# A decoder layer on one core: modulation and first latents in halves, earlier norms, later rope tables

## The chip, the cores and the metric

The kernel runs on one core of one Trainium2 chip. The metric is the time of one execution in device microseconds, from the first to the last instruction with the little that lies around them. The engines are PE (TensorE; PEld is its loading of weights), DVE (VectorE), ACT (ScalarE), POOL (GpSimd) and SP (SyncE, which issues most transfers).

## What is computed

One decoder layer on 512 rows of width 1024. The part that the change touches is the very beginning: six modulation vectors from a conditioning vector, a normed and modulated input, and the low-rank query latents of its projection.

```python
mod = silu(c) @ w_ada + b_ada                    # 6 vectors of 1024
shift1, scale1, gate1, shift2, scale2, gate2 = mod
h = rms_norm(x, norm1_g) * (1 + scale1) + shift1
proj = h @ w_in                                  # split: cq, ckv, kpe, fq, fk, fv, fl
q_a = rms_norm(cq, mla_qa_g) @ w_uq              # 8 heads, latent attention with rope
kv_a = rms_norm(ckv, mla_kva_g) @ w_ukv
# attention of both groups, o @ w_o, gate1, residual
# second norm and modulation, 8 heads of product keys, top 16 of 16384 experts, gate2, residual
```

## The kernel before

The 512 rows are four tiles of 128. Every tile's row block is transposed to eight blocks of 128 features, so a product with an input matrix runs over eight k blocks. Products that need accuracy are made of three (`mm3`, L380 to L387): both operands are split into an upper part in the fast float format and a lower part, the rest, and upper·upper, upper·lower and lower·upper are summed in one PSUM bank. `halves` (L364) loads a weight matrix in blocks of two k, casts the upper part on ACT (L373) and subtracts on DVE (L374).

The modulation is computed from `w_ada`, 512 columns at a time: `wload` (L283) loads a half vector's matrix in four blocks of 512 KB, `mod_parts` (L298) multiplies, and the second step of `mod_cols` (L307) turns the sums into columns, 4 of the 8 columns of `a1` (scale times gain) or `b1` (shift). So `a1` and `b1` come in two halves, each for four of the eight k blocks.

`hidden` (L400) makes one tile's modulated rows. Its first step loads x and norms it (`normed_T`, L340: Square on ACT with the sum, a reciprocal root on GpSimd, a scaling on DVE). Its second step transposes all eight blocks, applies `a1` and `b1` (`scaled`, L156: even blocks on ACT, odd ones on DVE) and splits the result (`part`, L393: upper part on ACT; lower part of blocks 0 to 3 on DVE, of 4 to 7 on GpSimd). `latent_q` (L412) multiplies with `w_c0` (384 columns, 24 products a tile) and norms; `latent_k` (L424) does it with `w_c1` (296 columns); then come `w_fv`, `w_fk`, `w_fq` (512 columns each).

The order is written out at the end of `build`: a list of steps (L1068), in which only tiles 0 and 1 are taken through `hidden`, then `tables` (L206), which calls `rope_tables` (L233), then `pipe` (L63) over the tasks, which starts one task a tick and resumes each three ticks later. Tiles 2 and 3 are the first two tasks. From this program order a scheduler makes a fixed list of instructions for each engine at build time; each engine then runs its list in order. It may put an instruction earlier in an engine's list than the program has it, if its inputs are there by the scheduler's own estimate.

Buffers: the pool `k4` (L93) has 28 slots of 4 KB a partition for x, the normed rows `xn`, the split rows `hT`, raw and split weights and the modulation's blocks; `ld` has 4, `k3` has 6, PSUM has 6 banks named `bank` and 2 named `bank2`. A transfer into a slot waits until the slot's former content has been used.

Of the kernel before, what the change touches and what calls it, by code (L numbers as in the profile page):

```python
# [17 lines left out]
OP = mybir.AluOpType  # L18
# [3 lines left out]
P = 128  # L22
S = 512
D = 1024
KD = D // P
# [53 lines left out]
class Layer:  # L79
# [75 lines left out]

    def scaled(self, dst, a, b=None):  # L156

        def f(j, n, p):
            for q in range(n):
                d, s, x = dst(j + q), p[:, q, :], j + q  # L160
                if x % 2:
                    if b is None:
                        self.nc.vector.tensor_scalar(d, s, a[:, x:x + 1], None, op0=OP.mult)
                    else:
                        self.nc.vector.tensor_scalar(d, s, a[:, x:x + 1], b[:, x:x + 1], op0=OP.mult, op1=OP.add)
                else:
                    self.nc.scalar.activation(d, s, AF.Identity, scale=a[:, x:x + 1],
                                              bias=0.0 if b is None else b[:, x:x + 1])
        return f
# [36 lines left out]
    def tables(self):  # L206
# [23 lines left out]
        self.logf = [cp.tile([P, H], F32, name=f"logf{i}") for i in range(NT)]  # L230
        self.rope_tables()

# [106 lines left out]

    def normed_T(self, dst, x, a, b):  # L340

        nc = self.nc
        h = self.k4([P, D], "xn")
        ss, rstd = self.sm([P, 1], "nss"), self.sm([P, 1], "nrs")
        nc.scalar.activation(h, x, AF.Square, accum_out=ss)
        self.rsqrt(rstd, ss, 1, 1.0 / D)
        nc.vector.tensor_scalar(h, x, rstd, None, op0=OP.mult)
        yield
        self.transposes([h[:, k * P:(k + 1) * P] for k in range(KD)], self.scaled(dst, a, b))
# [13 lines left out]

    def halves(self, name, src, raw, new):  # L364

        if name not in self.wt:
            kd, n = src.shape[1:]
            his, los = [], []
            for k in range(0, kd, 2):
                w = raw([P, 2, n], "w")  # L370
                self.last_load = self.nc.sync.dma_start(w, src[:, k:k + 2, :])
                hi, lo = new([P, 2, n], "whi", F32R), self.k4([P, 2, n], "wlo", F32R)
                self.nc.scalar.copy(hi, w)  # L373
                self.nc.vector.tensor_tensor(out=lo, in0=w, in1=hi, op=OP.subtract)  # L374
                his += [hi[:, x, :] for x in range(2)]
                los += [lo[:, x, :] for x in range(2)]
            self.wt[name] = his.__getitem__, los.__getitem__
        return self.wt[name]

    def mm3(self, pb, lhs, rhs, kd):  # L380

        pe = self.nc.tensor
        for k in range(kd):
            (lh, ll), (rh, rl) = (tuple(f(k) for f in t) for t in (lhs, rhs))
# [3 lines left out]

    def w_in(self, name):

        return self.halves(name, self.I[name], self.k4, self.ld if name in ("w_c1", "w_fk") else self.k4)

    def part(self, f, hl, engs):  # L393

        for q in range(0, KD, 4):
            hi, lo, src = (t[:, q:q + 4] for t in (*hl, f))
            self.nc.scalar.copy(hi, src)
            engs[q // 4].tensor_tensor(out=lo, in0=src, in1=hi, op=OP.subtract)

    def hidden(self, i, T):  # L400
        nc = self.nc
        x = self.k4([P, D], "x")
        self.load(x, self.I["x"][i * P:(i + 1) * P, :])
        f = x.rearrange("p (k t) -> p k t", k=KD)
        yield from self.normed_T(lambda k: f[:, k, :], x, self.mods["a1"], self.mods["b1"])
        T["hT"] = [self.k4([P, KD, P], "hT" + z, F32R) for z in "hl"]
        self.part(f, T["hT"], (nc.vector, nc.gpsimd))

    def times_h(self, pb, i, T, name):
        self.mm3(pb, [lambda k, z=z: T["hT"][z][:, k, :] for z in range(2)], self.w_in(name), KD)  # L410

    def latent_q(self, i, T):  # L412
        nc, v = self.nc, self.nc.vector
        pq = self.bank()
        self.times_h(pq[:, :QR], i, T, "w_c0")
        T["cl"] = cl = self.k3([P, QR + KVR], "cl")
# [580 lines left out]
    def build(self):  # L997
# [57 lines left out]
        def gates(i):  # L1055
# [3 lines left out]
        each = lambda f, *a: [f(i, T[i], *a) for i in every]  # L1059
        base = (each(self.latent_q) + each(self.latent_k) + each(self.fox_v) + each(self.fox_qk, 0)  # L1060
                + each(self.fox_qk, 1) + each(self.mla_tile))
        hs = [self.hidden(i, T[i]) for i in every]
        for x in ("a1", "b1", "a2", "b2"):
            self.mods[x] = self.cp.tile([P, KD], F32, name=x)
        m = [f for half in range(2) for f in (self.mod_cols(0, "b1", 0, None, True, (half,)),
                                              self.mod_cols(1, "a1", 1, 4, True, (half,)))]
        h0, h1 = hs[:2]
        for g in (m[0], h0, h1, m[1], m[0], m[2], m[1], m[3], m[2], m[3], h0, h1):  # L1068
            next(g, None)
        self.tables()  # L1070
        mods = spread(seq(self.mod_row(2, 0, self.g1d), self.mod_cols(3, "b2", 2), self.mod_cols(4, "a2", 3, 5),
                          self.mod_row(5, 1, self.g2d)), 2)
# [4 lines left out]
                    spread(q1(2), 2), top(0, 2))  # L1077
        tasks = hs[2:] + base + self.heads(0, T)
        skip = len(tasks) + 10
# [83 lines left out]
```

## Time and profile before

| | us |
|---|---|
| median of 3 runs | 1729.67 |
| lowest and highest | 1727.96, 1730.6 |
| the profiled execution | 1727.06 |
| its span, first to last instruction | 1725.3 |
| busy in the span: PE, DVE, ACT, POOL | 1594.3, 1251.7, 679.0, 470.3 |

A busy time is a sum of marks; PE's marks overlap, so a busy PE need not be at its peak. The granted clock is a share of 2.4 GHz: 1.00 is 2.4 GHz, 0.50 is 1.2 GHz. In rows of the timeline the start stands first, then the time, engine and line, the output and the input, and in brackets the engine's idle time before the row and what ended it. An engine's name with q (SPq, ACTq) is its issue of a transfer.

### The profile page before, as it was taken

What the parts mean: (1) busy time and instruction counts of PE and PEld (TensorE: products, weight loads), DVE (VectorE), ACT (ScalarE), POOL (GpSimd) and SP (SyncE); (2) the same over time, 40 slices, a digit from 0 to 9 for tenths busy, and PEclk for the clock granted to TensorE, in tenths of its full rate; (3) what the DMA queues carried; (4) which work ended last, traced back from release to release, by engine and by line L of the source; (5) the groups of instructions that cost most, each with busy time, mean ns of one, the idle gap of its engine ahead of it and who ended that gap; (6) DMA issues with size and microseconds to landing.
All of it is one profiled execution on the core that took longest, in us unless ns stands there. A gap on an engine that the chain in (4) does not pass through costs nothing.

```text
span 1725.3 us, 24991 instructions
## 1 busy us (share of the span) xinstructions
PE 1594.3 (92%) x8993; PEld 1398.1 (81%) x8993; DVE 1251.7 (73%) x2626; ACT 679.0 (39%) x1072; POOL 470.3 (27%) x506
## 2 busy tenths in 40 slices
PE   5999999888985999999999999689999999999996
PEld 2976498876985999999999999677777777777885
DVE  3524454476799888778878787488888788888863
ACT  3522364335321544334656565333333333333331
POOL 1203500000033345533112111133433234343421
PEclk8999999899996999999999999889999999999998
DMA  7355413347325888888999999899999999999963
GB/s 289 119 208 185 164 46 111 110 153 255 118 94 201 268 257 263 269 262 264 317 297 317 305 300 300 295 362 399 363 356 376 373 367 374 363 372 378 311 197 105
DMA packets 189904, 451.34 MB, mean 262 GB/s; under 512 B 16595, under 2 KB 102611, under 8 KB 185685
## 3 DMA queue, kind: packets, MB, share of 16 engines
q1 hardware_dynamic: 92884, 279.27, 45.8%
q0 software_dynamic: 38016, 137.38, 22.8%
q10 hardware_dynamic: 58880, 33.11, 6.4%
q8 instruction: 70, 1.15, 0.3%
q14 instruction: 54, 0.43, 0.1%
HBM read 393.07 MB, written 56.63 MB: 261 GB/s over the span
## 4 chain that ended last, share of the span: by engine, by line
PE 60%; DVE 4%; DMA 3%; ACT 1%; issue 1%; POOLq 0%; POOL 0%; DVEq 0%; ACTq 0%; SPq 0%
PE acc L978 30%; PE bank L934 9%; PE bank L933 9%; PE bank L932 9%; PE bank L817 2%; DMA G<-gst 1%; DVE ulo L869 1%; DMA ge<-ged 1%; ACT vhi L868 1%; DVE scr L846 0%; DMA gt<-G 0%; DVE idf L770 0%; DVE vlo L869 0%; DMA g<-g2d 0%; DMA x<-xd 0%
## 5 line engine op out<-in xcount | busy, mean ns | idle before, releaser
L978 PE MATMUL acc<-vhi,whl 128*128 128x512 f32 x1536 | 421.8, 394 | 38.5 <-ACT whl L968 20.0
L978 PEld LDWEIGHTS acc<-vhi,whl 128*128 128x128 f32 x1536 | 288.5, 189 | 107.2 <-ACT vhi L868 23.7
L932 PE MATMUL bank<-hhi,uhi 128*128 128x384 f32 x1024 | 345.7, 338 | 21.0 <-DMA hhi<-hd 17.5
L934 PE MATMUL bank<-hhi,ulo 128*128 128x384 f32 x1024 | 347.0, 339 | 9.8 <-DVE ulo L869 9.7
L933 PE MATMUL bank<-hlo,uhi 128*128 128x384 f32 x1024 | 347.9, 340 | 0.2 <-DMA hlo<-hd 0.2
L868 ACT CAST uhi<-ut 128x1024 fp32r<-128x1024 f32 x128 | 134.5, 1051 | 305.2 <-PE bank L933 297.7
L828 POOL DMA_INDIRECT gat<-in_peer_v,ids x128 | 158.7, 1240 | 343.6 <-DVE y L856 314.0
L828 POOL DMA_INDIRECT gat<-in_peer_u,ids x128 | 141.5, 1106 | 385.4 <-DVE sact L846 355.1
L978 PE MATMUL acc<-vlo,whl 128*128 128x512 f32 x768 | 240.8, 395 | 3.4 <-DVE vlo L869 3.4
L869 DVE TENSOR_TENSOR ulo<-ut,uhi 128x1024 fp32r<-128x1024 f32 x128 | 177.7, 1388 | 77.8 <-ACT uhi L868 77.7
L932 PEld LDWEIGHTS bank<-hhi,uhi 128*128 128x128 f32 x1024 | 193.9, 189 | 22.4 <-issue 17.6
L934 PEld LDWEIGHTS bank<-hhi,ulo 128*128 128x128 f32 x1024 | 194.0, 189 | 13.2 <-DVE ulo L869 12.9
L933 PEld LDWEIGHTS bank<-hlo,uhi 128*128 128x128 f32 x1024 | 193.9, 189 | 1.1 <-DMA hlo<-hd 0.7
L868 ACT CAST vhi<-vt 128x1024 fp32r<-128x1024 f32 x128 | 133.8, 1049 | 142.2 <-PE acc L978 126.2
L869 DVE TENSOR_TENSOR vlo<-vt,vhi 128x1024 fp32r<-128x1024 f32 x128 | 156.6, 1223 | 43.2 <-ACT vhi L868 42.8
L978 PEld LDWEIGHTS acc<-vlo,whl 128*128 128x128 f32 x768 | 144.6, 189 | 36.9 <-DVE vlo L869 5.6
L856 DVE SCALAR_TENSOR_TENSOR y<-gat,swgt,y 128x1024 f32<-128x1024 f32 x127 | 166.7, 1313 | 2.2 <-DMA gat<-in_peer_v,ids 2.1
L968 ACT CAST whl<-ge 128x384 fp32r<-128x384 f32 x128 | 65.2, 511 | 249.6 <-PE acc L978 224.9
L846 DVE CUSTOM_DVE_ANT_0 scr<-gat,h2r 128x1024 bf16<-128x1024 f32 x128 | 157.3, 1229 | 0.8 <-DMA gat<-in_peer_u,ids 0.8
L969 DVE TENSOR_TENSOR whl<-ge,whl 128x384 fp32r<-128x384 f32 x128 | 70.6, 556 | 51.4 <-ACT whl L968 51.2
L819 ACT ACTIVATE gst<-bank 128x512 f32<-128x512 f32 x96 | 96.7, 1115 | 0.1
L965 DVE TENSOR_TENSOR ge<-ge,gt 128x384 f32<-128x384 f32 x128 | 69.4, 554 | 23.3 <-DMA gt<-G 16.7
(251 smaller groups left out, 2232.9 us busy)
## 6 DMA issues: line engine op xcount, KB each, us to landing
ut<-in_peer_uT SPq DMA_DIRECT2D x128, 512.0 KB, 5.0
vt<-in_peer_v SPq DMA_DIRECT2D x128, 512.0 KB, 6.8
G<-gst ACTq DMA_DIRECT2D x24, 1024.0 KB, 9.9
gt<-G SPq DMA_DIRECT2D x16, 1536.0 KB, 9.5
ged<-ge SPq DMA_DIRECT2D x120, 192.0 KB, 4.3
ge<-ged SPq DMA_DIRECT2D x120, 192.0 KB, 6.9
w<-in_w_ada SPq DMA_DIRECT2D x16, 1024.0 KB, 7.2
w<-in_w_pq SPq DMA_DIRECT2D x32, 512.0 KB, 5.2
```

Source lines behind the costliest of these rows:

```text
L819: nc.scalar.activation(st[:, :, q + t4:q + t4 + 4].rearrange("p i t -> p t i"), pb.rearrange("p (t i) -> p t i", t=4), AF.Copy, scale=1.0 ...
L828: self.nc.gpsimd.indirect_dma_start(out=t, out_offset=None, in_=self.I[table], in_offset=bass.IndirectOffsetOnAxis(ap=ids[:, k:k + 1], axi ...
L846: v.tensor_tensor_reduce(out=scr, in0=u, in1=self.rows, op0=OP.mult, op1=OP.add, scale=1.0, scalar=0.0, accum_out=a[:, k:k + 1])
L856: v.scalar_tensor_tensor(out=self.y, in0=t, scalar=w[:, k:k + 1], in1=self.y, op0=OP.mult, op1=OP.add)
L868: nc.scalar.copy(hi, src)
L869: self.last_split = eng.tensor_tensor(out=lo, in0=src, in1=hi, op=OP.subtract)
L932: pe.matmul(A, uh[:, k, :], hh, start=(k == 0), stop=False)
L933: pe.matmul(A, uh[:, k, :], hl, start=False, stop=False)
L934: pe.matmul(A, ul[:, k, :], hh, start=False, stop=(k == KD - 1))
L965: nc.vector.tensor_tensor(out=wg, in0=wg, in1=self.gt[:, :, b % GI, :], op=OP.mult)
L969: nc.vector.tensor_tensor(out=wl, in0=w, in1=wh, op=OP.subtract)
L978: self.nc.tensor.matmul(self.acc[t][half], w[:, ts], v[:, half * 512:(half + 1) * 512], start=(b == n == 0), stop=(b == NK - 1 and n == 2))
```

## The change

Six things are changed. `hidden` has three steps: norm; transposes, modulation and split of blocks 0 to 3; the same of blocks 4 to 7. `latent_q` has its products in two steps, over k blocks 0 to 3 and 4 to 7, into the same bank. `w_in` can load just the first part of a matrix. The written order takes all four tiles through the norm beside the first half of the modulation, loads the first half of `w_c0` ahead of the second half of the modulation, does the first halves of all tiles' rows and latents before the second half of the modulation is turned into columns, and then the second halves. The lower part of the split is always taken on DVE (it was on GpSimd for blocks 4 to 7). `rope_tables` is no longer called in `tables`; it is a task of its own behind the latents. The number of tasks falls by one.

```diff
-    def scaled(self, dst, a, b=None):
+    def scaled(self, dst, a, b=None, k0=0):
@@ tables
         self.logf = [cp.tile([P, H], F32, name=f"logf{i}") for i in range(NT)]
-        self.rope_tables()
@@ halves
-    def halves(self, name, src, raw, new):
+    def halves(self, name, src, raw, new, upto=None):
...
+        his, los = self.wt[name]
+        if len(his) < (upto or kd):
+            for k in range(len(his), upto or kd, 2):
                 w = raw([P, 2, n], "w")
                 self.last_load = self.nc.sync.dma_start(w, src[:, k:k + 2, :])
...
@@ mm3
-        for k in range(kd):
+        for k in ks or range(kd):
...
@@ hidden
-        yield from self.normed_T(lambda k: f[:, k, :], x, self.mods["a1"], self.mods["b1"])
+        h = self.norm(x)
+        yield
         T["hT"] = [self.k4([P, KD, P], "hT" + z, F32R) for z in "hl"]
-        self.part(f, T["hT"], (nc.vector, nc.gpsimd))
+        for q in range(0, KD, 4):
+            self.transposes([h[:, k * P:(k + 1) * P] for k in range(q, q + 4)],
+                            self.scaled(lambda k: f[:, k, :], self.mods["a1"], self.mods["b1"], q))
+            hi, lo, t = (z[:, q:q + 4] for z in (*T["hT"], f))
+            nc.scalar.copy(hi, t)
+            nc.vector.tensor_tensor(out=lo, in0=t, in1=hi, op=OP.subtract)
+            yield
@@ latent_q
-        self.times_h(pq[:, :QR], i, T, "w_c0")
+        self.times_h(pq[:, :QR], i, T, "w_c0", range(KD // 2))
+        yield
+        self.times_h(pq[:, :QR], i, T, "w_c0", range(KD // 2, KD))
@@ build
-        h0, h1 = hs[:2]
-        for g in (m[0], h0, h1, m[1], m[0], m[2], m[1], m[3], m[2], m[3], h0, h1):
+        lq = [self.latent_q(i, T[i]) for i in every]
+        for g in (m[0], *hs[:2], m[1], *hs[2:], m[0], m[1]):
+            next(g, None)
+        self.w_in("w_c0", KD // 2)
+        for g in (m[2], m[3], *hs[:2], *lq[:2], *hs[2:], *lq[2:]):
+            next(g, None)
+        self.w_in("w_c0")
+        for g in (m[2], m[3], *hs):
             next(g, None)
         self.tables()
+        base = (lq + [prep(self.rope_tables)] + each(self.latent_k) + each(self.fox_v) + each(self.fox_qk, 0)
+                + each(self.fox_qk, 1) + each(self.mla_tile))
...
-        tasks = hs[2:] + base + self.heads(0, T)
+        tasks = base + self.heads(0, T)
```

## Rows read from the trace of the kernel before

**Rows 1.** The page's strip of 40 slices: busy tenths of PE
```profile
PE   5999999888985999999999999689999999999996
```

**Rows 2.** PE's waits from 0 to 45 us: total, times, longest
```profile
PE bank L385 <- ACT whi L373: 9.7, 1, 9.7
```

**Rows 3.** Stretches: length, busy PE, PEld, DVE, ACT, POOL, granted clock, DMA share, GB/s
```profile
20.00:31.20 11.20, 10.28 (x70) 4.32 (x68) 5.25 (x20) 4.30 (x9) 0.00 (x0) 1.00 1.03 407
31.00:32.00 1.00, 0.19 (x2) 0.10 (x1) 0.62 (x5) 0.37 (x2) 0.00 (x0) 0.78 1.05 410
31.20:40.80 9.60, 0.00 (x0) 0.00 (x0) 3.20 (x17) 5.72 (x13) 3.07 (x4) 0.52 0.40 140
40.80:48.70 7.90, 7.46 (x24) 6.63 (x25) 6.47 (x11) 4.91 (x10) 1.51 (x4) 0.50 0.31 90
48.70:63.50 14.80, 14.80 (x89) 14.77 (x89) 6.58 (x11) 5.45 (x14) 5.52 (x8) 1.00 0.30 94
63.50:76.60 13.10, 13.10 (x98) 13.10 (x98) 4.87 (x19) 6.62 (x21) 4.10 (x17) 1.00 0.64 238
110.00:200.00 90.00, 87.58 (x422) 57.58 (x422) 35.58 (x54) 23.96 (x38) 32.19 (x48) 1.00 0.59 216
```

**Rows 4.** Timeline from 20 to 45 us, single rows of several engines
```profile
20.10 2.77 PE L303 MATMUL bank<-w,c 128*32 128x512 f32 x20
20.69 1.67 SPq L281 DMA_DIRECT2D x<-in_x  x2
23.30 21.15 SPq L371 DMA_DIRECT2D w<-in_w_c  x6
24.35 0.81 ACT L167 ACTIVATE x<-bank,b,a 128x128 f32<-128x128 f32 x2 [1.71 <-DVE a L321]
27.12 0.69 DVE L398 TENSOR_TENSOR hTl<-x,hTh 128x512 fp32r<-128x512 f32 x1 [0.34 <-ACT hTh L397]
28.40 1.05 PE L303 MATMUL bank<-w,c 128*32 128x512 f32 x4 [0.23 <-DMA w<-in_w_ada]
29.50 0.33 ACTq L243 DMA_DIRECT2D rg<-in_rope_g  x1
31.63 0.81 ACT L167 ACTIVATE x<-bank,b,a 128x128 f32<-128x128 f32 x2 [1.55 <-DVE a L321]
35.34 0.23 DVE L276 SCALAR_TENSOR_TENSOR rope<-ropework,rg 128x64 f32<-128x64 f32 x1 [2.46 <-DMA rg<-in_rope_g]
36.87 1.14 ACT L397 CAST hTh<-x 128x512 fp32r<-128x512 f32 x2 [3.45 <-DVE x L165]
37.56 2.49 POOL L398 TENSOR_TENSOR hTl<-x,hTh 128x512 fp32r<-128x512 f32 x2 [22.28 <-ACT hTh L397]
37.91 1.05 ACT L345 ACTIVATE xn<-x 128x1024 f32<-128x1024 f32 x1
40.01 0.81 ACT L373 CAST whi<-w 128x768 fp32r<-128x768 f32 x1
40.87 1.01 PE L385 MATMUL bank<-whi,hTh 128*128 128x384 f32 x2 [9.69 <-ACT whi L373]
```

**Rows 5.** Timeline of PE from 45 to 64 us, single rows
```profile
45.59 0.52 PE L387 MATMUL bank<-whi,hTl 128*128 128x384 f32 x1
47.19 0.52 PE L387 MATMUL bank<-whi,hTl 128*128 128x384 f32 x1
52.89 1.04 PE L136 MATMUL bank<-ident,xn 128*128 128x128 f32 x8
60.91 0.34 PE L385 MATMUL bank<-whi,hTh 128*128 128x384 f32 x1
63.51 0.30 PE L385 MATMUL bank<-whi,hTh 128*128 128x296 f32 x1
```

**Rows 6.** SP's waits from 0 to 66 us, and issues from 44 to 48 us (median to landing)
```profile
SPq L371 <- POOL hTl L398: 11.6, 2, 10.5
...
w<-in_w_c SPq DMA_DIRECT2D x2, 296.0 KB, 2.8
```

More of the change, by code (lines that the diff above doesn't have):

```diff
@@ L154, in apart @@
         return f
-    def scaled(self, dst, a, b=None):
+    def scaled(self, dst, a, b=None, k0=0):
         def f(j, n, p):
             for q in range(n):
-                d, s, x = dst(j + q), p[:, q, :], j + q
+                d, s, x = dst(k0 + j + q), p[:, q, :], k0 + j + q
                 if x % 2:
@@ L338, in mod_row, with norm @@
         yield
-    def normed_T(self, dst, x, a, b):
+    def norm(self, x):
         nc = self.nc
@@ L347, in normed_T @@
         nc.vector.tensor_scalar(h, x, rstd, None, op0=OP.mult)
+        return h
+    def normed_T(self, dst, x, a, b):
+        h = self.norm(x)
         yield
@@ L362, in weights1 @@
         return self.wt[name, 1]
-    def halves(self, name, src, raw, new):
+    def halves(self, name, src, raw, new, upto=None):
+        kd, n = src.shape[1:]
         if name not in self.wt:
-            kd, n = src.shape[1:]
-            his, los = [], []
-            for k in range(0, kd, 2):
+            self.wt[name] = ([], [])
+        his, los = self.wt[name]
+        if len(his) < (upto or kd):
+            for k in range(len(his), upto or kd, 2):
                 w = raw([P, 2, n], "w")
@@ L376, in halves, with mm3 @@
                 los += [lo[:, x, :] for x in range(2)]
-            self.wt[name] = his.__getitem__, los.__getitem__
-        return self.wt[name]
-    def mm3(self, pb, lhs, rhs, kd):
+        return his.__getitem__, los.__getitem__
+    def mm3(self, pb, lhs, rhs, kd, ks=None):
         pe = self.nc.tensor
-        for k in range(kd):
+        for k in ks or range(kd):
             (lh, ll), (rh, rl) = (tuple(f(k) for f in t) for t in (lhs, rhs))
@@ L387, in mm3, with w_in @@
             pe.matmul(pb, ll, rh, start=False, stop=(k == kd - 1))
[L389 to L398, printed above, removed]
+    def w_in(self, name, upto=None):
+        return self.halves(name, self.I[name], self.k4, self.ld if name in ("w_c1", "w_fk") else self.k4, upto)
     def hidden(self, i, T):
@@ L404, in hidden, with times_h @@
         f = x.rearrange("p (k t) -> p k t", k=KD)
-        yield from self.normed_T(lambda k: f[:, k, :], x, self.mods["a1"], self.mods["b1"])
+        h = self.norm(x)
+        yield
         T["hT"] = [self.k4([P, KD, P], "hT" + z, F32R) for z in "hl"]
-        self.part(f, T["hT"], (nc.vector, nc.gpsimd))
-    def times_h(self, pb, i, T, name):
-        self.mm3(pb, [lambda k, z=z: T["hT"][z][:, k, :] for z in range(2)], self.w_in(name), KD)
+        for q in range(0, KD, 4):
[5 more added lines that the diff above has]
+            yield
+    def times_h(self, pb, i, T, name, ks=None):
+        self.mm3(pb, [lambda k, z=z: T["hT"][z][:, k, :] for z in range(2)], self.w_in(name, ks and ks[-1] + 1), KD, ks)
     def latent_q(self, i, T):
@@ L1059, in build @@
         each = lambda f, *a: [f(i, T[i], *a) for i in every]
-        base = (each(self.latent_q) + each(self.latent_k) + each(self.fox_v) + each(self.fox_qk, 0)
-                + each(self.fox_qk, 1) + each(self.mla_tile))
         hs = [self.hidden(i, T[i]) for i in every]
```

## The prediction

> **What bounds the kernel now.** I read the page first. Its strip of 40 slices has PE at nine tenths or more nearly everywhere after the first slice, so whatever shortens PE's work list or its early idle time moves the end, unless a later wait gives it back [rows 1]. The change touches only the front, so I then read PE's waits there and the table of stretches. One wait stands out: the first product of the query latents waits 9.7 us, for the upper part of its weights, cast on ACT [rows 2]. From 31.2 to 40.8 PE does nothing, from 40.8 to 48.7 it works at clock 0.50, and from 48.7 on it is full at clock 1.00: 14.80 of 14.80 us, then 13.10 of 13.10 [rows 3]. In the stretch from 110 to 200 it is still busy 87.58 of 90. So the front is bound by loading and norming up to about 41 us, and after 48.7 by PE alone.
>
> Why 41? Read the timeline in order [rows 4]. The last matrix block of the modulation lands at 28.4 (PE waited for it), its columns are ready when ACT starts to scale tile 0's second half at 31.63: 3.2 us. There the chain breaks: DVE took the rope tables in first and stood until 35.34 for the small rope load, which ACT's queue issued at 29.50. So the cast of tile 0's modulated rows starts only at 36.87. Behind it on ACT stand the norms of tiles 2 and 3 (37.91, two of 1.05 and their accumulator reads), and only then the weights' cast at 40.01, though the weights had been asked for from 23.30 on. GpSimd's share of the split took 2.49 us as well. The clock had fallen by then (0.78 in the microsecond from 31, 0.50 afterwards) and it came back at about 48.7 [rows 3].
>
> The mark that I count by is the end of the query latents on PE: the first 296-column product of the next step begins at 63.51 [rows 5]. Everything before that mark (tiles 2 and 3 included) is the same work after the change. What comes behind it is PE-bound and starts when it starts, so the gain is the shift of this mark, less what the hand-over costs.
>
> **The change, part by part.**
>
> *Loads.* DMA runs at 407 GB/s in this stretch with a share of 1.03 [rows 3], so order is all that can change. Today x of tiles 2 and 3 goes out at 20.69 and w_c0 at 23.30, behind all modulation blocks [rows 4]. Afterwards two tiles of x (2 x 512 KB) and half of w_c0 (2 x 384 KB) go ahead of the second half of the modulation: 1.835 MB at 0.407 MB per us = 4.5 us. The last modulation block lands at 28.4 + 4.5 = 32.9. The front up to the first halves of a1 and b1 stays as it is: ACT begins to scale with them at 24.35 [rows 4].
>
> *First halves.* Eight k blocks become two times four, so half of the latents' 96 products (48) can run while the modulation still loads. Each half tile costs ACT 0.81 + 0.57 = 1.4 us (two scalings of 0.81 together, half of the 1.14 for two casts) and DVE as much (0.76 for its two scalings, which is ACT's order of size, and 0.69 for the split) [rows 4]. Four half tiles from 24.35 on are ready by about 30. The 48 products take 0.173 us each (15 of them from 60.91 to 63.51 [rows 5]), 8.3 us. PE is marked busy 10.28 of 11.2 us from 20 on, but marks overlap: 20 records of modulation products follow one another in 2.77 us [rows 4], 0.14 each, so the second half of the modulation (32 records) needs 4.4 us of PE in the 14.7 us that it and the loads ahead of it now take (10.2 by the old landings, and 4.5). Room of 10.3 us against 8.3 of products and 2.1 of transposes: I take it that they just fit and cost nothing. If this cover is gone, they cost up to 8.3 us (a rival below).
>
> *Norms.* All four tiles are normed as they land: 2.5 us of ACT leave the path between 37.9 and 40.0. The split of the lower part goes to DVE (0.69) from GpSimd (2.49 for two). Nothing is late for it: GpSimd is busy 3.07 of 9.60 us there, most of it this [rows 3].
>
> *Rope.* The wait from 31.63 to 36.87 goes. The tables' small DVE operations (some 20 of 0.2 us, 4 us in all, by the row at 35.34 [rows 4]) and the small loads that they issue on ACT's queue now stand behind the latents and ahead of latent_k's weights. DVE has room: busy 6.58 of 14.80 and 4.87 of 13.10 [rows 3]. If DVE again stood for the rope load, the splits of w_c1 would be queued behind it, and PE behind those. Bounds for this hand-over: nothing (the tables fill a hole in DVE, as their first half did before), and 4 us (a wait like the present 2.5 us and half of the operations). The present steps of that hand-over, cast 0.68 and split 0.77, run without a PE wait, so I take 1.
>
> *Second halves.* First scaling at 32.9 + 3.2 = 36.1; + 0.81 + 0.57 gives the first product at 37.5. The remaining w_c0 half lands about 1.9 us after 32.9 and is cast by then. PE then has 48 x 0.173 = 8.3 us, and about 1.0 for eight of the sixteen half-tile transposes (1.04 for eight [rows 5]; the others fit ahead). ACT and DVE need 1.4 us a tile, PE 2.1, so PE is the limit: 46.8 at full clock.
>
> *Clock.* The trace has no such stretch. From 32.9 to 37.5 PE has only the last block's products, the column products and transposes: what it had around 30 before, when the clock fell at 31 to 32. I expect the fall again. The clock came back 7.8 us after the first latent product (40.87), in a stretch that still had holes (7.46 busy of 7.90) [rows 3, 4]; the new stream will have none, so I take less, 5 us at half clock, where products start every 0.32 us (five from 45.59 to 47.19 [rows 5]): 2.5 us lost. Bounds: 0 and the whole stretch at half clock, 48 x 0.147 = 7.1. The mark then stands at 46.8 + 2.5 = 49.3.
>
> Here a rule speaks against the change. The Trainium skill (TensorE: Matmul & The Clock Gate, section "HAM oscillation — how this bites in real kernels") advises to do all K tiles of an output before waiting for a DMA, so that PE stays warm; the change cuts K in two with a load between. By that rule all second halves would run cold; the trace shows half clock behind a load wait, but also the return within 7.8 us. By the one the mark is 53.9, by the other 49.3.
>
> *Sum.* 63.5 - 49.3 = 14.2, less 1 for the hand-over: 13.2 us. The profiled execution's own time is 1727.06 (span 1725.3 and 1.8 around it), which would become 1713.9. It lies 2.6 below the median of the runs, so on their scale: 1729.67 - 13.2 = **1716.5**.
>
> **The rivals.**
>
> *The clock stays full.* Filled with first halves, PE never gives it up. The mark is at 46.8, gain 15.7: 1714.0. For it: clock 1.00 from 20 to 31 with PE filled. Against it: the fall after the same chain at 31.6.
>
> *All second halves at half clock.* 46.8 + 7.1 = 53.9, gain 8.6: 1721.1. Against it: the return at 48.7. (The page named above speaks for it, and no more than that hangs on the page.)
>
> *First halves come late.* PE takes its work in a fixed order. If they stand behind the last modulation products, they start at 32.9 + 1.1 = 34.0 and end at 42.3; the second halves end 8.3 + 1.0 later, at 51.6, at full clock since PE never stops: gain 10.9, 1718.8; with 2.5 of half clock 1721.3.
>
> *The pool of 28 slots runs full, and this is the case that can end slower.* With all four tiles in flight x, xn and two hT each take 16 slots, w_c0's parts 8, the mask 1: 25. SP already stood 10.5 us for a slot of hT before [rows 6]. If the blocks of the next matrix are served one by one, each costs its landing 2.8 [rows 6], cast 0.68 and split 0.77, 4.3 us, where PE uses one in 13.1 / 4 = 3.3: 4.3 + 3 x 1.0 = 7.3 us. For w_c1 alone the gain shrinks to 5.9 (1723.8). For w_fv's larger blocks it would be some 8.5 more by the same count, together 15.8: 1732.3, and through w_fk 1741. It decides from the point where two matrices are served so. Against it: in the present stretch from 48.7, with the pool as full, PE waits for nothing. A change of order further back, from the same slots, I count here.
>
> That the change does nothing would need the front not to be bound as read; the 9.7 us wait speaks against it.
>
> **How the numbers follow.** Forecast 45% (1716.5), full clock 15% (1714.0), all cold 10% (1721.1), late first halves 12% (1718.8 to 1721.3), one matrix served singly or as much given back later 8% (1724 to 1729), more than that 10% (1732 and up). A measurement of this kernel tells about 0.2% (3.5 us) from no change. Faster 0.82, within that 0.08, slower 0.10. The range, from full clock with no hand-over cost and a few us of spread to the end of the one-matrix case: 1710 to 1727.
>
> **What would show it.** Right: rope's DVE operations behind the latents; norms of four tiles before 30; 384-column products before 33; the last modulation block at about 33; second halves from about 37.5; the first 296-column product at 48 to 51; PE without waits from there to 110. Wrong: PE idle behind that mark for a cast or split, SP waiting long for slots, or the distance of 13 us shrinking between 110 and 560.

## The result: slower, and the profile after

The changed kernel takes 1737.26 us in the median of six runs (1733.96 to 1743.48), the kernel before beside it 1727.78: a ratio of 1.0057, 95% interval 1.0035 to 1.008, so 6 to 14 us slower. The forecast was 1716.5 with a range up to 1727; it missed on the wrong side. The profiled execution took 1734.92 us, its span is 1733.2.

In the text below the **mark** is the first 512-column product, of `fox_v`: 77.4 us before, 85.5 after (+8.1). The first 296-column product, by which the prediction counted, stood at 63.5 and now at 68.2, but in some of the experiments single 296-column products are moved up into holes, so it is no fair mark between kernels.

PE's waits after, from 0 to 110 us (total, times, longest), against [rows 2]:

```profile
PE bank L302 <- DMA w<-in_w_ada: 6.2, 2, 5.5
PE bank L390 <- ACT whi L379: 4.9, 1, 4.9
PE bank L136 <- DVE xn L346: 3.7, 1, 3.7
PE bank L390 <- ACT hTh L410: 3.2, 1, 3.2
PE bank L136 <- DVE cl L442: 1.9, 1, 1.9
```

The wait of 9.7 us for the weights of the first latent product is gone, as meant. In its place stand 3.2 us for the first half tile (L410), and further back 1.5 ahead of the second halves (the row at 53.88 below), 4.9 us for weights again (L379), now those of `w_c1`, and 1.9 us for normed latents. The stretches after, columns as in [rows 3]:

```profile
20.00:30.00 10.00, 6.30 (x29) 2.38 (x29) 4.35 (x11) 6.30 (x12) 1.48 (x4) 0.67 1.03 409
30.00:40.00 10.00, 9.82 (x41) 5.19 (x43) 4.80 (x9) 4.50 (x10) 0.00 (x0) 0.80 0.36 122
40.00:50.00 10.00, 10.00 (x50) 5.89 (x48) 1.92 (x2) 1.71 (x3) 0.00 (x0) 1.00 0.28 76
60.00:80.00 20.00, 15.12 (x96) 14.78 (x95) 9.74 (x31) 4.85 (x11) 2.10 (x6) 0.91 0.44 159
80.00:100.00 20.00, 18.07 (x99) 15.41 (x99) 14.40 (x87) 10.67 (x34) 6.42 (x20) 1.00 0.01 1
```

PE is idle now between 20 and 30 (6.30 of 10) instead of between 31 and 41, and again between 60 and 80 (15.12 of 20), where it was full [rows 3]. What PE does in the front is the main reading. Single rows of its timeline:

```profile
30.18 0.69 PE L390 MATMUL bank<-whi,hTh 128*128 128x384 f32 x1 [3.19 <-ACT hTh L410]
31.11 1.92 PE L302 MATMUL bank<-w,c 128*32 128x512 f32 x4
36.44 1.05 PE L302 MATMUL bank<-w,c 128*32 128x512 f32 x4
37.42 0.62 PE L392 MATMUL bank<-whi,hTl 128*128 128x384 f32 x2
45.89 1.05 PE L302 MATMUL bank<-w,c 128*32 128x512 f32 x4
46.87 0.45 PE L390 MATMUL bank<-whi,hTh 128*128 128x384 f32 x1
49.60 1.84 PE L317 MATMUL bank<-o,macc 128*128 128x1 f32 x16
53.88 1.09 PE L136 MATMUL bank<-ident,xn 128*128 128x128 f32 x8 [1.50 <-DVE x L165]
54.72 0.42 PE L390 MATMUL bank<-whi,hTh 128*128 128x384 f32 x1
62.99 0.34 PE L392 MATMUL bank<-whi,hTl 128*128 128x384 f32 x1
```

The second half of the modulation (L302) is no block any more: seven groups of four records, at 31.11, 36.44, 37.97, 39.87, 41.93, 44.18 and 45.89, stand between the latents' first-half products. Its last one starts at 45.89, where before it was over by 29.5 [rows 4], although PE waited for none of its data after 11 us. Only then come the columns (L317, 49.60), the scaling, and the second halves, from 54.72 to 63.2. So the query latents end at 63.3, just where they ended before (63.5 [rows 5]). The hand-over behind them, rows of three engines:

```profile
63.38 0.33 ACTq L242 DMA_DIRECT2D rg<-in_rope_g  x1
63.69 0.64 DVE L248 TENSOR_SCALAR ropework<-frq,posf 128x16 f32<-128x16 f32 x4
67.18 0.40 ACT L264 ACTIVATE ropework<-ropework 128x64 f32<-128x64 f32 x2 [3.23 <-DVE ropework L263]
67.49 3.38 ACT L379 CAST whi<-w 128x592 fp32r<-128x592 f32 x5
68.21 1.35 PE L390 MATMUL bank<-whi,hTh 128*128 128x296 f32 x4 [4.88 <-ACT whi L379]
68.42 0.22 DVE L276 TENSOR_TENSOR rope<-ropework,rg 128x64 f32<-128x64 f32 x1
68.56 3.96 DVE L380 TENSOR_TENSOR wlo<-w,whi 128x592 fp32r<-128x592 f32 x5
```

The rope tables run on DVE from 63.69 to 68.6. ACT has their sine (L264) ahead of the casts of `w_c1` (L379) and stands 3.23 us for DVE; DVE has the splits (L380) behind them. From the last 384-column product (62.99) to the mark (85.52) it takes 22.5 us. Before, it took 14.1.

### The profile page after: what moved, and what is told of

The parts are those of the page before. It is cut to its first block, busy times and chain, and to the rows that moved or that the text cites. A ratio compares the mean times of both kernels' runs of the same rounds, so it can differ in the third digit from the quotient of the medians.

```text
span 1733.2 us, 25000 instructions
## 1 busy us (share of the span) xinstructions
PE 1598.7 (92%) x8993; PEld 1397.3 (81%) x8993; DVE 1252.6 (72%) x2630; ACT 679.8 (39%) x1072; POOL 455.6 (26%) x502
## 4 chain that ended last, share of the span: by engine, by line
PE 79%; DVE 11%; DMA 5%; issue 2%; ACT 2%; POOL 0%; POOLq 0%; DVEq 0%; ACTq 0%; SPq 0%
PE acc L985 30%; PE bank L941 9%; PE bank L940 9%; PE bank L939 9%; PE bank L173 4%; PE bank L391 2%; PE bank L390 2%; PE bank L824 2%; PE bank L392 2%; PE bank L136 2%; PE bank L571 2%; PE bank L302 2%; PE bank L586 1%; DMA G<-gst 1%; DMA keys<-in_keys 1%
## 5 line engine op out<-in xcount | busy, mean ns | idle before, releaser
L941 PE MATMUL bank<-hhi,ulo 128*128 128x384 f32 x1024 | 346.9, 339 | 14.7 <-DVE ulo L876 14.6
L835 POOL DMA_INDIRECT gat<-in_peer_v,ids x128 | 153.1, 1196 | 344.5 <-DVE y L863 314.9
```

The lines of the kernel that those rows point to most:

```text
L835: self.nc.gpsimd.indirect_dma_start(out=t, out_offset=None, in_=self.I[table], in_offset=bass.IndirectOffsetOnAxis(ap=ids[:, k:k + 1], axi ...
L941: pe.matmul(A, ul[:, k, :], hh, start=False, stop=(k == KD - 1))
```

## The experiments

The theory: two things were mis-seen, each on a list that an engine runs in order. On PE the modulation is broken up between the first halves, so the second halves come late (**mixing**). On ACT and DVE the rope tables stand ahead of `w_c1`'s casts and splits (**rope**). Rivals: the halves are slow by themselves (clock, half tiles); or the loss is further back, in the order of loads.

Starts on PE in the profiled execution of each run (us), and the ratio of the runs to those of the kernel before beside them:

| run | last modulation product | last 384-column product | mark | Ratio, 95% interval |
|---|---|---|---|---|
| before | 28.9 | 63.3 | 77.4 | |
| after | 46.3 | 63.0 | 85.5 | 1.0057 (1.0035 to 1.008) |
| e1_rope_back | 46.6 | 65.6 | 78.8 | 1.0033 (1.0016 to 1.005) |
| e2_rope_late | 46.0 | 65.5 | 78.8 | 1.009 (1.0073 to 1.0107) |
| e3_hold_first | 35.2 | 56.7 | 79.4 | 1.0023 (1.0014 to 1.0033) |
| e4_hold_rope_late | 35.7 | 62.5 | 74.2 | 1.0045 (1.0029 to 1.0062) |
| e15_new_mods20 | 44.5 | 61.1 | 83.7 | 1.0069 (1.0052 to 1.0086) |
| e14_mix_rope_mods20 | 46.6 | 66.1 | 79.5 | 1.0029 (1.0016 to 1.0042) |
| e8_hold_rope_mods20 | 35.7 | 62.2 | 74.0 | 1.0001 (0.9991 to 1.0011) |
| e10_two_and_two | 37.6 | 65.2 | 77.0 | 1.001 (0.9998 to 1.0021) |
| e6_old_rope_lq | 29.0 | 57.0 | 78.5 | 1.0076 (1.0059 to 1.0093) |
| e5_old_rope_late | 31.9 | 59.2 | 72.9 | 1.0044 (1.0027 to 1.006) |
| e9_old_mods21 | 32.4 | 63.4 | 77.4 | 1.0008 (0.9998 to 1.0017) |
| e11_old_rope_mods22 | 30.4 | 57.0 | 70.7 | 0.9993 (0.9979 to 1.0008) |
| e16_old_cast_early | 30.0 | 62.0 | 75.7 | 1.0013 (1.0004 to 1.0023) |
| e17_old_delay | 29.6 | 63.5 | 83.1 | 1.0052 (1.0039 to 1.0065) |

Each start is of one execution, and it varies: where nothing ahead of a point was edited, two executions differ by up to 3.5 us at the last modulation product (before and e9) and up to 2.2 at the mark (e5 and e11; after and e15 1.8). So a difference of 2 us between two marks shows nothing by itself. In e1, e2, e4, e8, e10, e14 products of `latent_k` are mixed into the end of the 384-column ones (in e17 some of the added products), so there the mark alone compares.

**The hold (e3).** The first halves of the latents are issued behind the last product of the modulation on PE.

```diff
-            self.nc.tensor.matmul(pb[q:q + 32, :], ...)
+            self.last_mod = self.nc.tensor.matmul(pb[q:q + 32, :], ...)
...
-        for g in (m[2], m[3], *hs[:2], *lq[:2], *hs[2:], *lq[2:]):
+        for g in (m[2], m[3], *hs):
             next(g, None)
+        with self.tc.issue_after(self.last_mod.ins):
+            for g in lq:
+                next(g, None)
```

> The changed kernel, but with the first halves of the latents' products held on PE behind the last product of the modulation (48 products in a row instead of mixed with the modulation's). Theory (the mixing on PE, not the loads, held the second half of the modulation back from about 33 to 46.9 us): the last modulation product ends at 33 to 35 us, the query latents end at 53 to 56 instead of 63.2, and the time falls by 7 to 10 us, to about the kernel before, since the rope tables' price of about 8 stays. Rival (the second half of the modulation lands late, its slots being held): last modulation product after 40, end of the latents at 60 or later, time as the changed kernel's.

Measured 1732.6 us, ratio 1.0023. PE rows of e3:

```profile
33.86 1.91 PE L302 MATMUL bank<-w,c 128*32 128x512 f32 x12
35.70 0.44 PE L390 MATMUL bank<-whi,hTh 128*128 128x384 f32 x1
44.15 0.95 PE L317 MATMUL bank<-o,macc 128*128 128x1 f32 x8
47.53 1.09 PE L136 MATMUL bank<-ident,xn 128*128 128x128 f32 x8 [1.50 <-DVE x L165]
61.89 0.62 PE L390 MATMUL bank<-whi,hTh 128*128 128x296 f32 x1 [4.91 <-ACT whi L379]
```

In a row, twelve records of the modulation take 1.84 us to the next product; in the changed kernel four alone take 0.98 (36.44 to 37.42). Held back, the modulation is over 11 us earlier and the query latents 6.3 us earlier than after. The wait for `w_c1` stays at 4.9: mixing and rope are two separate losses. The halves aren't slow by themselves: the 48 products of the first ones take 8.45 us (35.70 to 44.15). Both gains are smaller than expected: the latents end at 56.7 instead of 53 to 56, and the time is some 5 us below the changed kernel's instead of 7 to 10.

**The rope tables' place (e1, e2).** e1 calls `rope_tables` in `tables` again; e2 puts its task behind `fox_v`.

```diff
# e2
-        base = (lq + [prep(self.rope_tables)] + each(self.latent_k) + each(self.fox_v) + each(self.fox_qk, 0)
+        base = (lq + each(self.latent_k) + each(self.fox_v) + [prep(self.rope_tables)] + each(self.fox_qk, 0)
```

> The changed kernel with the rope tables called from `tables` again, as before the change. Theory (two separate prices; the rope tables behind the latents cost 4.9 us of PE wait for the first cast of w_c1, a restart at half clock and 1.9 us of a later wait, together the 8 us by which the end moved): the end of the query latents stays near 63 us, the wait of 4.9 is gone, the first 512-column product starts at 77 to 79 instead of 85.5, and the time is 6 to 8 us below the changed kernel's, within 2 us of the kernel before. Rival (the pool of 28 slots is full and w_c1 comes late because SP waits for slots): the wait for w_c1's cast stays at 4 us or more and the time stays 6 us or more above the kernel before.

> The changed kernel with the rope tables still further back, behind the product that makes v. Theory: as with the tables called early, no wait for w_c1's cast, first 512-column product at 77 to 79, time within 2 us of the kernel before; if the tables at their old place hold up the scaling again, this one is a few us faster than that one. Rival (full pool): wait for w_c1's cast stays, time 6 us or more above the kernel before.

Both take the wait of 4.9 us away and bring the mark from 85.5 to 78.8. But in the time e1 keeps only part of that (1735.07, ratio 1.0033) and e2 nothing (1744.58, 1.009), where both were expected within 2 us of the kernel before: the gain is lost again behind the mark. In e1 PE stands there for weights of `w_fq`, which SP issued at 134.65:

```profile
140.94 0.80 PE L391 MATMUL bank<-whi,hTh 128*128 128x512 f32 x1 [5.82 <-ACT whi L380]
```

**Both (e4).** The edits of e3 and e2 together.

> Both edits: first halves held behind the modulation's last product and the rope tables behind v. Theory (two separate prices that add up, and everything behind the latents starts when they end): end of the latents at 53 to 56, no wait behind it, first 512-column product at 67 to 70, time 8 to 10 us below the kernel before (ratio 0.994 to 0.996). Rival (what is gained in front is given back by later waits, the weights of the next matrices coming from a full pool): first 512-column product at 67 to 70 but the distance shrinks behind it, time within 3 us of the kernel before.

A miss. The mark is at 74.2, 3.1 us ahead of before, and the time is 1736.73, ratio 1.0045. Rows of SP, PE, DVE and ACT, and the longest of SP's waits from 50 to 125:

```profile
55.15 41.54 SPq L290 DMA_DIRECT2D w<-in_w_ada  x4
96.74 0.47 SPq L280 DMA_DIRECT2D rowb<-in_rows  x1
97.30 0.53 SPq L377 DMA_DIRECT2D w<-in_w_fk  x1
...
102.77 1.92 PE L302 MATMUL bank<-w,c 128*32 128x512 f32 x16
104.33 0.69 DVE L335 TENSOR_TENSOR row<-bank,rowb 128x512 f32<-128x512 f32 x1 [9.16 <-DMA rowb<-in_rows]
107.95 0.40 ACT L264 ACTIVATE ropework<-ropework 128x64 f32<-128x64 f32 x2 [2.37 <-DVE ropework L263]
109.56 0.59 ACT L303 COPY macc<-bank 128x512 f32<-128x512 f32 x1 [1.21 <-issue]
110.20 2.08 PE L334 MATMUL bank<-macc,o 128*128 128x512 f32 x2 [5.50 <-ACT macc L303]
...
SPq L290 <- PE bank L302: 33.4, 2, 33.0
```

Here is the third list. SP issues in order too. The matrix blocks of the later modulation (for `g1`, `b2` and so on, whose tasks start ten ticks into the pipeline) wait for slots that products of the modulation on PE must free: 33 us. Behind them in SP's list stand the loads of `w_fk` and `w_fq`, and the small one of a row that is added to the modulation's sums (`rowb`, 96.74). It is this row that PE comes to feel in e4. DVE stands 9.16 us for it; the rope tables, now behind `fox_v`, follow on DVE; their sine (L264) stands on ACT ahead of the copy of the next sums (L303); and PE waits 5.50 us for that copy, though the products that it copies were done by 104.7. So the rope tables stand in front of something that PE needs at this place too. e2 has the same chain, with a wait of 5.62. SP's long issue of four blocks (55.15, 41.54 us) is there in the changed kernel too, from 67.44 for 37.23 us, and in the kernel before, from 62.77 for 32.81; there it just doesn't hurt. Each shift of the front moves SP's order against PE's.

**With the later modulation later (e15, e14, e8).** To take that list out, the later modulation starts at the twentieth tick: e15 is the changed kernel with this line alone, e14 is e2 with it, e8 is e4 with it.

```diff
-            elif n >= 10:
+            elif n >= 20:
                 next(mods, None)
```

> The changed kernel with only the later four modulation vectors started ten ticks later, as the run with the old front and eleven ticks (which was as fast as the kernel before). Theory (behind the latents the changed kernel keeps what its front lost, 8 us at the first 512-column product, of which the rope tables are 6.7): first 512-column product at 85 to 86, end of the projections 8 us behind the old front with the same start, time 6 to 10 us above the kernel before. Rival (the loss is made in SP's order between 75 and 170, not in the front): time within 3 us of the kernel before.

> The same with the rope tables behind v: the halves mixed on PE remain, the rope tables' place and SP's order are taken out. Theory: first 512-column product at 78 to 80, 6 to 7 us ahead of the run with the tables in the changed place and kept to the end: 5 to 8 us faster than that one, 0 to 3 above the kernel before, so that the mixed halves alone gain nothing. Rival (the tables cost only where w_fk is late as well): less than 2 us between the two.

> The kernel with first halves held and the rope tables behind v, and the later four modulation vectors started ten ticks later, so that the loads of w_fk and w_fq stand ahead of theirs in SP's list. Theory (SP stood 33 us for a slot that only a later modulation product frees, with w_fk queued behind it, and so the 3 us that the front had won by the first 512-column product became a loss of 4.8 by the end of the projections): no PE wait over 2 us from 75 to 170, the lead of 3 us at the first 512-column product is kept or grows, time 3 to 8 us below the kernel before. Rival (the pool of 28 slots itself is too full): w_fk's loads still come after 95 us and PE waits; time 5 us or more above the kernel before.

Now the parts separate: 1740.7 with mixing and rope as changed, 1734.27 with rope out of the way, 1728.64 with both mended. Rope's place costs 6.4 us, mixing 5.6, and without both the change is worth nothing (1.0001, 0.9991 to 1.0011). The first step is of the expected size, but e15 and e14 lie 12.7 and 6.2 us above the kernel before, more than expected: by itself, the later start doesn't help the changed kernel (1.0069 against 1.0057). That e8 would be 3 to 8 us below the kernel before was a miss in the time. In its trace no PE wait from 75 to 170 is over 2 us, and the lead grows, as expected, from 3.4 at the mark to 6.0 from 628 to 1104 us (times of the kernel before); its trace has 2 us of it left at the end, and the median of the runs none. The later start takes out SP's wait and the copy behind the sine at once, so what each of the two costs isn't told apart.

**Two and two (e10).** e8 with the first halves of only two tiles behind the modulation's products and of the other two behind its columns (`last_col` is the last product of L317), so that the columns' chain (PE, DVE, ACT) is covered.

```diff
# against e8
-                nc.tensor.matmul(pb[:, q:q + 1], ...)
+                self.last_col = nc.tensor.matmul(pb[:, q:q + 1], ...)
...
         with self.tc.issue_after(self.last_mod.ins):
-            for g in lq:
+            for g in lq[:2]:
                 next(g, None)
         self.w_in("w_c0")
-        for g in (m[2], m[3], *hs):
+        for g in (m[2], m[3]):
             next(g, None)
+        with self.tc.issue_after(self.last_col.ins):
+            for g in lq[2:]:
+                next(g, None)
+        for g in hs:
+            next(g, None)
```

> As the one with the later start, but only the first halves of two tiles stand between the modulation's last products and its columns, those of the other two behind the columns. Theory (with all four ahead of the columns, 8.3 us of products keep the second half of the modulation waiting, and PE then has holes of about 4 us while the second halves are scaled): end of the latents 2 to 4 us earlier than with all four ahead (52 to 54 us), time 2 to 4 us lower than that one's. Rival (PE is full in that stretch either way): the same time.

A miss: mark at 77.0 instead of earlier than e8's 74.0, ratio 1.001. The granted clock is 0.61 over 20 to 40 us here and 0.75 in e8; whether that alone made the difference is not separated.

**Parts of the change on the kernel before (e6, e5, e9, e11).** e6 moves only the rope task, to the changed kernel's place; e5 moves it behind `fox_v`; e9 only starts the later modulation at tick 21; e11 is e5 with the start at tick 22.

```diff
# e6
-        self.rope_tables()
...
-        base = (each(self.latent_q) + each(self.latent_k) + ...
+        base = (each(self.latent_q) + [prep(self.rope_tables)] + each(self.latent_k) + ...
```

> The kernel before with one part of the change alone: the rope tables as a task between the latents and latent_k. Theory (the tables at that place stand on DVE and ACT ahead of the casts of w_c1): the front gains the 3.5 us for which ACT waited on DVE behind the rope load, the end of the latents comes at 58 to 61 us instead of 63.3, then PE waits about 5 us for the first cast of w_c1, the first 512-column product starts at 77 to 81 instead of 77.4, and the time is within 4 us of the kernel before. Rival (the tables are cheap there, and the changed kernel's wait comes from the rest of the change): no wait behind the latents, 3 to 5 us faster than the kernel before.

> The kernel before with the rope tables alone moved, behind v. Theory (in front the tables hold ACT up for 3.5 us on the scaling's path, behind v they hold nobody up, but SP then queues w_fk behind the later modulation): end of the latents at 57 instead of 63.3 us, no wait behind it, first 512-column product at 71 to 73, half or more of the 5 to 6 us given back by the end of the projections; time 0 to 4 us below the kernel before. Rival: the tables cost as much behind v as behind the latents; 5 us or more above.

> The kernel before with the later four modulation vectors started eleven ticks later and nothing else. Theory (in the kernel before PE never waits for w_fk, so their order is worth nothing there): within 2 us of the kernel before. Rival (the later start is a gain by itself): 3 us or more faster, and then what the neighbouring run gains is not the front's.

> The kernel before with the rope tables behind v and the later modulation started twelve ticks later. Theory: first 512-column product at 71 to 73, and the lead of 5 to 6 us kept to the end: 4 to 7 us below the kernel before, the fastest of all so far. Rival (a lead in front is given back further on whatever SP's order): within 2 us of the kernel before.

e6 is the cleanest test of the prediction's rope step. The latents end 6.3 us earlier (57.0), which confirms that the front waited for the rope load [rows 4]; and the hand-over takes it all back:

```profile
62.22 1.26 PE L384 MATMUL bank<-whi,hTh 128*128 128x296 f32 x4 [4.87 <-ACT whi L372]
```

The mark is 1.1 us late and the time 1.0076, more than expected; SP's order had changed as well (the last three blocks of `w_fk` at 112.52). e5 has the mark at 72.9, 4.5 early, and is still slower (1.0044, where 0 to 4 us faster was expected), with a PE wait of 6.42 us for weights at 111.49 behind a late `w_fk`, which SP issued at 106.19, behind the loads and the row of the later modulation. e9 shows that the later modulation's start alone is worth nothing. e11 mends e5: mark at 70.7, 6.7 early, the earliest of all, without any halves. Its median is 1726.38 against 1728.03, where 4 to 7 us less were expected, and the interval of its ratio takes in 1. Beside e8, which has the rope tables in the same place, its mark is 3.3 us earlier, but from 628 to 1104 us e8 is 6.0 us ahead of the kernel before and e11 only 3.0, and the intervals of their ratios overlap. So whether the halves bring or cost anything once the rope is out of the way stays open.

**A larger lead, and a plain delay (e16, e17).** e16 is e11 with `w_c0` cast ahead of the norms of tiles 2 and 3 and the whole split on DVE. e17 is the kernel before with 48 more products ahead of `latent_k`'s first; the real ones overwrite their results.

```diff
# e16, added to e11
-        self.part(f, T["hT"], (nc.vector, nc.gpsimd))
+        self.part(f, T["hT"], (nc.vector, nc.vector))
...
             next(g, None)
+        self.w_in("w_c0")
         self.tables()
# e17
+        if i == 0:
+            for _ in range(24):
+                for k in range(2):
+                    nc.tensor.matmul(pk[:, :n1], T["hT"][0][:, k, :], ..., start=True, stop=True)
```

> The kernel before with the rope tables behind v and the later modulation from step 22 on (as in the run with both), and besides w_c0 cast ahead of the norms of the third and fourth token tile on ScalarE, and GpSimd's half of the split of hT given to VectorE. First latent product between 34 and 37 instead of 40.8, first 512-column product at 67 to 69.5 (77.4 before). If a lead of the front passes to the end (theory): 3 to 7 us below the kernel before, ratio 0.996 to 0.998. If leads are given back by waits on casts and transfers further back (rival): within 2 us of it, as the 6.7 us lead of the run with both was.

> The kernel before with 48 more 296-column products on TensorE just ahead of latent_k's first product; the real products overwrite their results, so they only cost time: 48 x 0.137 us = 6.6 us of PE, with no other order, wait or transfer changed. If everything behind the mark moves with it, as the prediction had it (theory): the first 512-column product 6 to 7 us later than 77.4, the time 5 to 8 us above the kernel before run beside it (ratio 1.003 to 1.0045). If slack further back takes up a shift of the front (rival): the mark as late, the time within 2 us of the kernel before.

e16 is a miss in the front. The first latent product starts at 32.2, but the mark is at 75.7, later than in e11. Rows of e16:

```profile
45.70 1.97 PE L136 MATMUL bank<-ident,xn 128*128 128x128 f32 x8 [2.54 <-DVE xn L346]
50.28 0.69 PE L384 MATMUL bank<-whi,hTh 128*128 128x384 f32 x1 [2.62 <-ACT hTh L396]
...
40.00:60.00 20.00, 14.84 (x71) 14.03 (x70) 8.94 (x18) 10.65 (x24) 4.16 (x10) 0.74 0.24 73
```

The hole moved: with the casts ahead of the norms, tiles 2 and 3 came late (PE 14.84 of 20, clock 0.74). So e16 says nothing of a larger lead; its ratio is 1.0013.

e17 did what it was made for. The mark moves by 5.7 (6 to 7 were expected), the shift is 5.2 from 628 to 1104 us, and the time is 1737.1 against 1729.05: ratio 1.0052, 7 to 11 us. No task and no load was moved; a few of the added products went in among the latents'. A delay of the front reaches the end in full; nothing further back absorbs it. In the trace the shift is 10 us at the end; most of what is added, 4.2 us, comes between 1272 and 1568 us and isn't explained. So the 8.1 us at the changed kernel's mark, which are 8.1 at 1107 us too, are enough for its 9.5.

## Why the prediction was wrong, step by step

**What bounds the front: right.** The wait on the rope load was real (e6 and e11: the latents end 6.3 us earlier without it). That the kernel behind the mark is PE-bound held for a loss (e17).

**Loads: right, as far as seen.** After 11 us PE waited for none of the blocks. In e3 the last product of the modulation starts at 35.18 without a wait, so the last block, forecast for 32.9, had landed by then.

**First halves: the step that failed first.** "Room of 10.3 us against 8.3 of products and 2.1 of transposes: I take it that they just fit and cost nothing." The room was counted over all of the 14.7 us up to the last block at 32.9, but the same paragraph has the half tiles ready by about 30 (measured: first product at 30.18). Of those 14.7 us, 3 were left by then. And the list on PE is fixed: the products that didn't fit stood not behind the modulation, as the rival "first halves come late" had it, but between its products, so they held up what the second halves wait for. From 30.18 to 49.60 PE did 48 products (8.3 us by 0.173), seven groups of modulation (6.9 by 0.98), eight transposes (0.9), and lost another 3.3, part of it to the half clock in which it began (0.80 in 30 to 40). The second halves began at 54.7 and not at 37.5. Expected from this step and those beside it were 14.2 us at the end of the latents; there were 0.3.

Even in the order of that rival (e3) the latents end at 56.7 and not at 51.6. The first halves begin at 35.70 and not at 34.0. And the columns' products stand behind the first halves on PE (44.15 in the rows of e3), so the chain from them to the first scaled and split half tile, 3.2 and 1.4 us by the prediction's own rows, isn't covered. The sum had taken it as running beside the first halves. So the forecast gain was out of reach in this order too: in e8, with mixing and rope both mended, the second halves begin at 50.23 and not at 37.5, and the mark comes 3.4 us early and not 13.2.

**Norms: done early, at a price.** The norms and the casts of `w_c0` now stand on ACT ahead of the first half tile's cast, in rows from 24 to 30:

```profile
24.80 1.06 ACT L344 ACTIVATE xn<-x 128x1024 f32<-128x1024 f32 x1
27.14 0.83 ACT L379 CAST whi<-w 128x768 fp32r<-128x768 f32 x1
28.70 0.83 ACT L379 CAST whi<-w 128x768 fp32r<-128x768 f32 x1
29.51 1.14 ACT L410 CAST hTh<-x 128x512 fp32r<-128x512 f32 x2
```

PE waits 3.2 us for the last of them, and the clock falls there (0.67 in 20 to 30, where it was 1.00 [rows 3]). The prediction had said that the front up to the first halves of `a1` stays as it is.

**Rope: mis-sized.** Taken at 1, bounded by 4; measured 8.4 (22.5 us from the last 384-column product to the mark, against 14.1). Not the rope load made it: it was issued at 63.38, and no DVE row waits for it. Nor were the blocks of `w_c1` late: SP had issued all four by 52. It is 4.9 us of PE's wait, which ends with ACT's first cast, 1.9 for the latents' norm on DVE, and the remaining 1.6 for the most part the half clock in which PE starts again:

```profile
68.21:71.50 3.29, 3.29 (x14) 3.27 (x15) 3.29 (x9) 2.66 (x4) 0.00 (x0) 0.50 0.94 315
```

In e1, with the tables back at their old place, there is neither wait, and the clock is 1.00 from 60 to 80. The splits themselves are fast enough (3.96 us for five, where PE needs one in 3.3). The prediction named the splits queued on DVE and overlooked the sine on ACT, ahead of the casts.

With 13.9 us lost in the front and 7.4 in the hand-over, the forecast gain of 13.2 becomes a loss of 8.1 at the mark, which is what the trace has.

**Second halves: the length right, the place wrong.** 54.72 to 63.2 is 8.5 us for 8.3 forecast.

**Clock: the place wrong.** In the changed kernel the second halves ran at full clock (a product every 0.17), and the half clock stands behind the two longer waits, ahead of the first halves and at the hand-over. In e8 it is where it was forecast, behind a wait of 2.70 us ahead of the second halves:

```profile
50.40:54.00 3.60, 3.60 (x13) 3.49 (x14) 2.87 (x7) 2.98 (x7) 0.00 (x0) 0.53 0.58 184
```

From 54 on the clock is 1.00 there. The Trainium skill (TensorE: Matmul & The Clock Gate, section "HAM oscillation — how this bites in real kernels") says of K tiles with a wait for a load between them that each starts cold, and e8 bears that out behind its wait, here one for DVE. That all second halves would run cold, as the prediction had it by that rule, neither kernel shows.

**What stands behind starts when the mark starts: half right.** A delay passes (e17). A lead doesn't in full: of e11's 6.7 us at the mark 5.1 are left at 351 us, 3.0 at 1100 and, in the median, 1.6 (from 3.6 gained to 1.4 lost by the interval). In e4 and e5 the later modulation is the place where it goes, by PE's wait for the copy behind the sine (e4) and for `w_fk` behind its loads (e5): its later start alone, worth nothing on the kernel before (e9), brings 1.0045 to 1.0001 and 1.0044 to 0.9993. The prediction had "a change of order further back" only inside the slots' rival, at 8 and 10%. For e8 and e11, without such a wait, it stays open. One hint: from 1200 to 1600 us the DMA share is 0.97 to 1.00 in all traces, and there single executions differ by 4 to 5 us (between 1272 and 1568 us e8, e11, e16 and e17 each lose 3 to 4 us to before's trace, after none). Whether their runs lose it in the same measure, the profiled executions can't say: that of e8 (1724.91) is the fastest of its ten runs, that of e11 (1728.34) 2 us above its median.

**The pool of 28 slots: not the cause.** The time lies where this rival had it (1732 and up), but for other reasons. SP did stand for slots that the late modulation held, from 20 to 125 us:

```profile
SPq L377 <- PE bank L302: 20.1, 3, 7.5
```

But PE waited for no block that was loaded late for it, and nowhere behind the mark for one of `w_fv`.

## What to carry to other kernels

Work that is to fill a wait must be ready when the wait begins: lay its ready time beside the room, and ask where each engine's fixed list puts it if it comes late; between the products of the very chain that it was to hide, it delays that chain. A task moved off one engine's critical place stands ahead of something on every engine that it uses: list the next instruction of each (ACT's casts as well as DVE's splits, and behind `fox_v` ACT's copy of the modulation's sums). And a transfer queue that runs in order ties stages far apart together, so a gain in the front is not counted until the loads issued behind it have been followed.

## What the runs showed of the hardware

Products of the modulation (128x512, each on 32 columns of the array) are cheap in a run and dear when a block of four records stands alone. Four records take 0.55 us in a run of 20 (2.77 [rows 4]) and 0.61 in the run of 12 (1.84, e3), but 0.98 where they stand between full-width products (36.44 to 37.42 after). The prediction priced them by the run. By these rows, breaking the modulation up into seven groups cost 2.6 us (7 x (0.98 - 0.61)).

The traces also show why. The first row is of the kernel before, the second of the changed one:

```profile
94.13 1.06 PE L303 MATMUL bank<-w,c 128*32 128x512 f32 x8
115.41 1.92 PE L302 MATMUL bank<-w,c 128*32 128x512 f32 x16
```

Eight records alone take 1.00 us to the next product (94.13 to 95.13), no more than four, and sixteen take 1.85 (115.41 to 117.26), no more than twelve. So records of two neighbouring blocks run side by side, on different columns of the array (`mod_parts` gives each k of four its own 32), and a block alone leaves half of that unused.

The Trainium skill (TensorEngine Tiling (Array Packing), section "Tiling Modes") says that the array is drained when the tiling mode changes. Here that can be only a small part: eight records more add 0.85 us (1.85 - 1.00), so of the 0.98 for four alone some 0.1 is left for both changes of mode, by this estimate, and the product behind them takes 0.1 more than its 0.17 (38.96 to 39.24).
